# A hybrid SSD and gated-MLP trunk on one core: the first stage by halves of the tokens, in a fixed order

## The chip, the core and the metric

The kernel runs on one NeuronCore of a Trainium2 chip. The metric is the time of one execution on the device in microseconds (us): the median of several runs. One execution was also profiled, and every row shown here is from that execution.

The core's engines each work through their own queue in order: TensorE (PE, matrix products and transposes; its weight loads are PEld), VectorE (DVE), ScalarE (ACT), GpSimd (POOL) and SyncE (SP, which here only issues loads and stores). PE writes its results to PSUM, eight banks of 128 x 512 float32.

## What is computed

Two layers on 512 tokens of width 1024, all in float32. The first layer mixes by a state-space scan (SSD), the second by a gated MLP; each is followed by a SwiGLU and a gated embedding. The change lies in the first projection of the first layer:

```python
def rmsnorm(x, w, eps=RMS_EPS):
    return x * rsqrt(mean(x * x, axis=-1) + eps) * w

def ssd_mixer(u, w_in, ...):                 # u = rmsnorm(h, norm_mix[0])
    zxbcdt = u @ w_in                        # 1024 -> 2048 (z) + 4096 (x, B, C) + 32 (dt)
    xbc = silu(causal_dwconv(xbc, conv_w, conv_b))
    dt = softplus(dt + dt_bias)
    a = -exp(a_log)
    y = ssd_scan(xs, dt, a, bm, cm) + xs * d_skip[:, None]     # chunks of 128 tokens, 8 groups
    return gated_rmsnorm(y, z, norm_w) @ w_out

h = x
for i in range(2):
    h = h + mixer_i(rmsnorm(h, norm_mix[i]))
    h = h + swiglu(rmsnorm(h, norm_ffn[i]), ...)
    h = h + sigmoid(rmsnorm(h, ple_gate_norm[i]) @ ple_w_gate[i]) * rmsnorm(p[i] @ ple_w_proj[i], ple_norm[i])
return rmsnorm(h, final_norm)
```

## The kernel before

**Products in three.** To keep float32 accuracy at the fast rate, each operand is split in a high part, rounded to a short float32 form by a copy on ACT, and a low part, the difference, made by a subtraction. A product is then three on PE (`mm3`): high by high (L265), weights' high by x's low (L266), weights' low by x's high (L267). Weights come in units of 128 columns for all 1024 rows: `wraw` as loaded, `whi` and `wlo` after the split (L68 on ACT, L70 on DVE, for the first two units on POOL), with three buffers each of `whi` and `wlo` and two of `wraw`. The activations are eight blocks of 128 rows by 512 tokens, `xh` and `xl` (tags xh0 to xh7, xl0 to xl7).

**The first stage.** x is loaded as four chunks of 128 tokens in two pieces each (`gh`, L222 and L223), then the first weights, then a row of small loads, all on SP's queue. For each chunk DVE sums the squares of one piece (L381), ACT of the other (L382); a square root and a reciprocal give `rtok`, one over the norm of each token. PE transposes x into seven banks and `on_rows` spreads rtok over the rows (`rs`, copied by DVE at L303). Then for each of the eight blocks: DVE scales the transposed x by the norm's weight and by rs (L395), ACT makes xh (L397) and keeps the unscaled block as the residual H (L400), DVE or POOL makes xl (L398). With these, PE makes the products of units 0 and 1, which are group 0's B and C; then it transposes three sets of small parameters to columns (`to_columns`, L364), makes dt's 32 columns from xh and xl by the unsplit weights `wdt` (the tile u, L627), and goes on with unit 2, group 0's first block of xs.

**After it.** One unit's products (24 of 128x512) follow another: xs, xs, z, z of group 0, then six units for each of the groups 1 to 7. Between them stand the pieces of the scan, started by counts (`tock`, twice in a unit). `decays` makes the cumulative sums from dt; `spread` transposes them, writes them to DRAM and group 0's scan loads them back broadcast to all rows (`csb` and `e`, L502 and L505). POOL multiplies e by C (L578) and makes xdd from xdt (L571), which PE reads for the states (L583).

**Who orders.** The code is traced once and a scheduler then orders each engine's instructions by priority and by estimates of their times; tiles are assigned to buffers and waits follow from the reads and writes. A block under `tc.high_priority` (the weights' splits are) moves ahead.

## Time and profile before

| what | value |
|---|---|
| median of 3 runs | 1576.19 us (1574.93 to 1577.48) |
| the profiled execution's own time | 1578.61 us |
| span of its trace, first to last instruction | 1576.9 us |
| PE busy | 1551.4 us, 98% of the span |
| DVE, ACT, POOL busy | 908.5 (58%), 643.7 (41%), 281.6 us (18%) |

The profiled execution is 2.4 us over the median, and 1.7 us of its time lie outside the span. [...] Of the span's first slice of 39 us PE is busy for seven tenths, of nearly all others for nine or more.

### The profile page before, as it was taken

Reading aid. Unit: us, or ns where it says so; the run is one execution under the profiler, and the core shown is the slowest. Engines: PE = TensorE matmul, PEld = TensorE weight load, DVE = VectorE, ACT = ScalarE, POOL = GpSimd, SP = SyncE. Lnnn points to the kernel's source line nnn. Section 1 sums busy time; section 2 is a strip of 40 time slices with the busy share of each in tenths; the row PEclk is TensorE's granted clock in tenths of the full one; section 3 lists DMA queues with packets and bytes.
Section 4 is the critical chain, followed back from the end, with each engine's and each line's share of the span. In section 5 each row is a group of like instructions: output and inputs, shape, how many; then the busy total and the mean of one; then the engine's idle time right before and its main releaser. Section 6 shows DMA issues by size and latency. Waiting matters only on the chain.

```text
span 1576.9 us, 18208 instructions
## 1 busy us (share of the span) xinstructions
PE 1551.4 (98%) x7348; PEld 1282.0 (81%) x7348; DVE 908.5 (58%) x1226; ACT 643.7 (41%) x843; POOL 281.6 (18%) x219
## 2 busy tenths in 40 slices
PE   7999999999999999999999999999999999999997
PEld 5878788888878788888888888888888888888886
DVE  5679895699886433433456647435554354433445
ACT  5556653466454222222344534323443242212336
POOL 2032220122254101100124200202221001101020
PEclk8999999999999999999999999999999999999999
DMA  6453453434424233233232333332232332333231
GB/s 181 113 139 108 127 127 104 111 121 121 140 81 133 87 102 107 81 107 96 78 120 81 107 92 102 96 111 88 87 107 83 105 101 86 107 92 95 81 107 54
DMA packets 151364, 164.15 MB, mean 104 GB/s; under 512 B 5320, under 2 KB 133872, under 8 KB 151280
## 3 DMA queue, kind: packets, MB, share of 16 engines
q1 hardware_dynamic: 149648, 157.74, 33.2%
q0 software_dynamic: 1600, 5.24, 1.2%
q8 instruction: 57, 0.93, 0.2%
q14 instruction: 27, 0.22, 0.1%
q10 hardware_dynamic: 32, 0.01, 0.0%
HBM read 160.75 MB, written 2.23 MB: 103 GB/s over the span
## 4 chain that ended last, share of the span: by engine, by line
PE 90%; DVE 5%; DMA 2%; ACT 1%; POOL 1%; issue 1%; SPq 0%; ACTq 0%; DVEq 0%; POOLq 0%
PE ps L265 28%; PE ps L266 28%; PE ps L267 28%; PE ps L872 1%; DVE wlo L70 1%; PE ps L527 1%; PE ps L260 1%; DVE acc L451 1%; DVE csb L511 1%; PE ps L583 1%; DMA csb<-cs_dram 1%; PE ps L529 1%; POOL sq L350 0%; DVE rs L283 0%; DVE csb L576 0%
## 5 line engine op out<-in xcount | busy, mean ns | idle before, releaser
L68 ACT ACTIVATE whi<-wraw 128x1024 fp32r<-128x1024 f32 (+1 forms) x270 | 279.0, 1038 | 698.6 <-PE ps L266 616.3
L265 PE MATMUL ps<-xh,whi 128*128 128x512 f32 x1120 | 442.4, 395 | 1.9 <-ACT h L400 1.9
L266 PE MATMUL ps<-xl,whi 128*128 128x512 f32 x1120 | 437.8, 391 | 2.9 <-DVE xl L398 2.0
L267 PE MATMUL ps<-xh,wlo 128*128 128x512 f32 x1120 | 437.8, 391 | 0.0
L70 DVE TENSOR_TENSOR wlo<-wraw,whi 128x1024 fp32r<-128x1024 f32 (+1 forms) x268 | 326.3, 1222 | 98.1 <-ACT whi L68 96.7
L265 PE MATMUL ps<-gh,whi 128*128 128x512 f32 x784 | 306.3, 391 | 0.0
L266 PE MATMUL ps<-gl,whi 128*128 128x512 f32 x784 | 305.0, 389 | 0.0
L267 PE MATMUL ps<-gh,wlo 128*128 128x512 f32 x784 | 304.9, 389 | 0.0
L265 PEld LDWEIGHTS ps<-xh,whi 128*128 128x128 f32 x1120 | 211.4, 189 | 48.9 <-issue 2.8
L266 PEld LDWEIGHTS ps<-xl,whi 128*128 128x128 f32 x1120 | 211.4, 189 | 47.3 <-DVE xl L398 2.5
L267 PEld LDWEIGHTS ps<-xh,wlo 128*128 128x128 f32 x1120 | 211.1, 188 | 44.5
L265 PEld LDWEIGHTS ps<-gh,whi 128*128 128x128 f32 x784 | 147.2, 188 | 30.7 <-issue 0.3
L606 DVE TENSOR_TENSOR h<-h,ps 128x512 f32<-128x512 f32 x88 | 60.0, 685 | 194.5 <-PE ps L267 194.4
L267 PEld LDWEIGHTS ps<-gh,wlo 128*128 128x128 f32 x784 | 147.2, 188 | 30.6
L266 PEld LDWEIGHTS ps<-gl,whi 128*128 128x128 f32 x784 | 147.3, 188 | 30.0
L752 POOL TENSOR_TENSOR zs<-zs,rs 128x512 f32<-128x512 f32 x44 | 74.1, 1687 | 545.9 <-ACT zs L751 545.9
L758 DVE TENSOR_TENSOR xsT<-ps,zs 128x512 f32<-128x512 f32 x44 | 30.4, 691 | 126.6 <-PE ps L267 117.9
L749 DVE TENSOR_TENSOR acc<-ps,rs 128x512 f32<-128x512 f32 x44 | 30.4, 690 | 108.2 <-PE ps L267 108.2
L350 POOL TENSOR_TENSOR sq<-sq,sq 128x512 f32<-128x512 f32 x43 | 65.7, 1528 | 131.3 <-ACT sq L347 129.4
L265 PE MATMUL ps<-whi,gh 128*128 128x512 f32 (+1 forms) x200 | 76.4, 382 | 0.0
L266 PE MATMUL ps<-wlo,gh 128*128 128x512 f32 (+1 forms) x200 | 76.2, 381 | 0.0
L267 PE MATMUL ps<-whi,gl 128*128 128x512 f32 (+1 forms) x200 | 76.1, 381 | 0.0
(293 smaller groups left out, 1419.6 us busy)
## 6 DMA issues: line engine op xcount, KB each, us to landing
wraw<-in_ffn_w_gate_dram SPq DMA_DIRECT2D x22, 1024.0 KB, 5.4
wraw<-in_ffn_w_up_dram SPq DMA_DIRECT2D x22, 1024.0 KB, 5.4
wraw<-in_ssd_w_in_dram SPq DMA_DIRECT2D x16, 1024.0 KB, 5.4
wraw<-in_ffn_w_down_dram SPq DMA_DIRECT2D x16, 1024.0 KB, 5.2
wraw<-in_gmlp_w_in_dram SPq DMA_DIRECT2D x16, 1024.0 KB, 5.5
wraw<-in_ssd_w_in_dram SPq DMA_DIRECT2D x16, 512.0 KB, 4.7
csb<-cs_dram SPq DMA_DIRECT2D x32, 256.0 KB, 4.4
wraw<-in_ple_w_gate_dram SPq DMA_DIRECT2D x8, 1024.0 KB, 5.1
```

The costliest lines, as they stand in the source:

```text
L68: nc.scalar.activation(hi, src, AF.Copy)
L70: (nc.vector if n > 1 else nc.gpsimd).tensor_tensor(lo, src, f32(hi), op=ALU.subtract)
L260: nc.tensor.transpose(ps, src, ident)
L265: mm(ps, wh, xh, start=start, stop=False)
L266: mm(ps, wh, xl, start=False, stop=False)
L267: mm(ps, wl, xh, start=False, stop=stop)
L350: nc.gpsimd.tensor_tensor(sq, sq, accum, op=ALU.add)
L451: stt(a[:, d:], ps[:, : S - d], pcols[:, 0, j * 32 + b : j * 32 + b + 1], a[:, d:], op0=ALU.mult, op1=ALU.add)
L606: tt(H[m], H[m], ps, op=ALU.add)
L749: tt(a, ps, rs, op=ALU.mult)
L752: nc.gpsimd.tensor_tensor(s, s, rs, op=ALU.mult)
L758: tt(t, ps, gate[m], op=ALU.mult)
```

## The change

The first stage is written anew, in an order that holds as written on every engine.

- **Halves of the tokens.** x's first two chunks are loaded, then the first weights, then the other two chunks, and unit 2's and 3's weights at once behind them. Scaling, xh, xl and H are made for tokens 0 to 255 for all eight blocks and then for tokens 256 to 511, in 128x256 pieces; the products of units 0 and 1 likewise, 96 of 128x256 for 48 of 128x512. The weights' low parts of these two units are made in halves, three on DVE and one on POOL.
- **A fixed order.** `in_order` ties each instruction in its block to the one traced before it on the same engine. Instructions from outside the block can still be put between them.
- **Idle transposes.** `warm(n)` has PE transpose the identity into a bank that nobody reads: 8 at the start, 4 and 8 around the row factors.
- **dt from H.** dt's products read H, without the norm, by weights that DVE has scaled by the norm's weights (L749): 8 products for 16. The token factor rtok is multiplied in afterwards, in `softplus`, which runs in the middle of the first xs unit.
- **Moved.** Small loads go to ACT's and POOL's queues; p's load goes from the start to group 2; the copy of d, the third set of columns, and `spread` (to the middle of group 1's first unit) are placed elsewhere; a square-root is done at the start, so that ACT's table for it is there.

```diff
+@contextmanager
+def in_order(tc):
+    traced = tc.nc.cur_bb.bb.instructions
+    last = traced[-1]
+    yield
+    prev = {}
+    for i in traced[next(k for k in reversed(range(len(traced))) if traced[k] is last) + 1 :]:
+        if i.engine in prev:
+            tc.add_manual_dep(i, prev[i.engine].name, mybir.DependencyInfo(
+                mybir.DependencyClass.NoSync, mybir.DependencyReason.DATA), reason="in_order")
+        prev[i.engine] = i
...
-            (nc.vector if n > 1 else nc.gpsimd).tensor_tensor(lo, src, f32(hi), op=ALU.subtract)
+            nc.vector.tensor_tensor(lo, src, f32(hi), op=ALU.subtract)
...
         x_tok.append((a, b))
-    W._load(0)
+        if c == 1:
+            W._load(0)
+    W._load(1)
...
-        q.dma_start(out=rowB[dst[0] : dst[1]], in_=src)
+        nc.gpsimd.dma_start(out=rowB[dst[0] : dst[1]], in_=src)
...
-    for c in range(NCH):
-        one = slice(c, c + 1)
...
-        for k in range(KD - 1):
-            tr_x(xT[k], k, c)
-    rs = on_rows(rtok, nc.vector.tensor_copy)
-    for k in range(KD):
...
+    def x_sums(c):
         stt(slot("e6"), x_tok[c][0], 1.0 / DM, x_tok[c][0], op0=ALU.mult, op1=ALU.mult, accum_out=ss2[:, c, 0:1])
         act(slot("e7"), x_tok[c][1], AF.Square, scale=1.0 / 32, accum_out=ss2[:, c, 1:2])
-        tt(ss[:, one], ss2[:, c, 0:1], ss2[:, c, 1:2], op=ALU.add)
+        tt(ss[:, c : c + 1], ss2[:, c, 0:1], ss2[:, c, 1:2], op=ALU.add)
...
+    def x_scale(hf, k):
+        src, cols = x_part(hf, k)
...
+        stt(tmps[k][:, cols], src, pcolN(k), rs0[:, cols], op0=ALU.mult, op1=ALU.mult)
+        act(Xh[k][:, cols], tmps[k][:, cols], AF.Copy)
+
+    def x_lo(hf, k, engine):
+        cols = slice(hf * HT, (hf + 1) * HT)
+        engine.tensor_tensor(Xl[k][:, cols], tmps[k][:, cols], f32(Xh[k][:, cols]), op=ALU.subtract)
+
+    def x_keep(hf, k):
+        src, cols = x_part(hf, k)
+        act(H[k][:, cols], src, AF.Copy)
...
+    def products(hf, n, k):
+        cols = slice(hf * HT, (hf + 1) * HT)
+        _, wh, wl = units[n]
+        mm3(first[n][:, cols], wh[:, k], wl[:, k], Xh[k][:, cols], Xl[k][:, cols], k == 0, k == KD - 1)
+
+    with in_order(tc):
+        warm(8)
+        to_columns(3, rowN, 16)
+        for c in range(2):
+            x_sums(c)
+            x_transpose(0, c, 0, KD)
+        x_rms(0)
+        x_rms(1)
+        warm(4)
+        x_rows(0)
+        warm(8)
+        unit_hi(0)
+        x_scale(0, 0)
+        x_lo(0, 0, G_)
+        unit_lo(0, V_, 0, 4)
...
+        for c in (2, 3):
+            x_transpose(1, c, 4, KD)
+        W.taken = 2
+        for k in range(KD):
+            x_scale(1, k)
+            x_lo(1, k, V_ if k in (0, 3, 6) else G_)
+            if k == 3:
+                W._split(2)
+            x_keep(1, k)
+            for n in range(2):
+                products(1, n, k)
...
+        to_columns(0, rowA, P)
+        to_columns(1, rowB, P)
+
+        tt(wdt, wdt, pcols[:, 3, :KD].unsqueeze(2).to_broadcast([P, KD, 32]), op=ALU.mult)
+    for m in range(2):
+        bc(m, first[m])
...
-        for n, x_ in enumerate((Xh, Xl)):
-            for j in range(4):
-                mm(ps[j * 32 : (j + 1) * 32], wdt[:, 2 * j + k], f32(x_[2 * j + k]), start=k + n == 0, stop=k + n == 2)
+        for j in range(4):
+            mm(ps[j * 32 : (j + 1) * 32], wdt[:, 2 * j + k], H[2 * j + k], start=k == 0, stop=k == 1)
...
+    gemm(1, KD, Xh, Xl, xs, tick=half)
...
     def tock():
+        if now[0] == 13:
+            spread()
...
-            if g == 1 and b == 0:
-                spread()
+            if g == 2 and b == 0:
+                load_p(0, [slot("e6"), slot("e7")])
```

Three places show how instructions stand now. The first is POOL's queue in the first stage, before: the two loads of p, the low parts of the two weight units, and three low parts of x.

```order
L254 DMA e6_82_470<-in_p_dram 128x2x256
L254 DMA e7_83_471<-in_p_dram 128x2x256
L70 TENSOR_TENSOR wlo0_283<-wraw0_113,whi0_282 128x1024
L70 TENSOR_TENSOR wlo1_287<-wraw0_113,whi1_286 128x1024
L398 TENSOR_TENSOR xl3_46_238<-e3_44_235,xh3_45_237 128x512
L398 TENSOR_TENSOR xl5_54_254<-e5_52_251,xh5_53_253 128x512
L398 TENSOR_TENSOR xl7_63_275<-acc_61_272,xh7_62_274 128x512
```

After, POOL's queue there has seven rows for the first half of the tokens, and the first of the second half behind them (e0 to e5 and acc are the scaled x).

```order
L440 TENSOR_TENSOR xl0_28_209<-e0_26_207,xh0_27_208 128x256
L440 TENSOR_TENSOR xl1_34_225<-e1_32_223,xh1_33_224 128x256
L665 TENSOR_TENSOR wlo0_205<-wraw0_105,whi0_204 128x512
L440 TENSOR_TENSOR xl3_42_246<-e3_40_244,xh3_41_245 128x256
L440 TENSOR_TENSOR xl5_50_279<-e5_48_277,xh5_49_278 128x256
L440 TENSOR_TENSOR xl6_58_311<-acc_56_309,xh6_57_310 128x256
L440 TENSOR_TENSOR xl7_62_318<-acc_60_316,xh7_61_317 128x256
```

The whole units have gone to DVE in three of four halves, and POOL has more and smaller subtractions of x.

The second place is the end of the stage on DVE. Before, the low parts of units 3 and 4 stand between the copies of the transposed parameters (pcols), and dt's result is copied (csb) behind them; nothing that dt's products read is made here.

```order
L398 TENSOR_TENSOR xl6_58_262<-acc_56_259,xh6_57_261 128x512
L365 COPY pcols_134<-ps_67_340 128x128
L70 TENSOR_TENSOR wlo3_391<-wraw1_280,whi3_390 128x1024
L70 TENSOR_TENSOR wlo4_398<-wraw2_384,whi4_397 128x1024
L365 COPY pcols_134<-ps_68_343 128x128
L365 COPY pcols_134<-ps_69_346 128x56
L628 COPY csb_75_365<-ps_76_366 128x512
```

After, the scaling of dt's weights (L749; u is wdt's tile) is the last row of the fixed order, and the same two low parts have been put ahead of it.

```order
L440 TENSOR_TENSOR xl6_58_311<-acc_56_309,xh6_57_310 128x256
L435 SCALAR_TENSOR_TENSOR acc_60_316<-ps_68_359,pcols_135,rs_14_139 128x256
L744 COPY cbm_3_94<-d2_125 16x128
L384 COPY pcols_135<-ps_69_453 128x128
L384 COPY pcols_135<-ps_70_456 128x128
L89 TENSOR_TENSOR wlo3_490<-wraw1_116,whi3_489 128x1024
L89 TENSOR_TENSOR wlo4_497<-wraw2_399,whi4_496 128x1024
L749 TENSOR_TENSOR u_13_127<-u_13_127,pcols_135 128x256
```

What dt's products read is thus made behind the low parts of units 3 and 4.

The third place is the end of the stage on PE, after: the last products of units 0 and 1 (banks ps_30 and ps_31), two transposes of parameters, dt's products by u from H, and the first product of xs.

```order
L284 MATMUL ps_31_216<-xh7_61_317,whi1_220 128x256
L285 MATMUL ps_31_216<-xl7_62_318,whi1_220 128x256
L286 MATMUL ps_31_216<-xh7_61_317,wlo1_221 128x256
L383 MATMUL ps_69_453<-ident_73,Btok_2_93 128x128
L383 MATMUL ps_70_456<-ident_73,cbm_3_94 128x128
L758 MATMUL ps_76_475<-h0_29_210,u_13_127 32x512
L758 MATMUL ps_76_475<-h2_39_236,u_13_127 32x512
...
L758 MATMUL ps_76_475<-h7_63_319,u_13_127 32x512
L284 MATMUL ps_79_500<-xh0_27_208,whi2_401 128x512
```

Between the last product of the stage and dt's there are only the two transposes, and xs stands behind dt, as it did before.

## Rows read from the trace of the kernel before

**Rows 1.** The page's part 1: engine, busy us, share, instructions.

```profile
PE 1551.4 (98%) x7348; PEld 1282.0 (81%) x7348; DVE 908.5 (58%) x1226; ACT 643.7 (41%) x843; POOL 281.6 (18%) x219
```

**Rows 2.** Waits of PE: who waited for whom, us in total, times, longest.

```profile
PE ps L266 <- DVE xl L398: 2.0, 1, 2.0
...
PE ps L583 <- POOL xdd L571: 1.6, 1, 1.6
```

**Rows 3.** Busy us by stretch: PE, PEld, DVE, ACT, POOL; clock, DMA share, GB/s.

```profile
11.00:14.00 3.00, 1.74 (x9) 0.88 (x8) 1.92 (x7) 2.17 (x6) 2.35 (x3) 0.97 1.06 268
14.00:19.00 5.00, 1.11 (x3) 0.51 (x3) 3.91 (x5) 2.93 (x5) 3.92 (x2) 0.50 0.57 130
19.00:24.00 5.00, 5.00 (x12) 3.91 (x13) 5.00 (x9) 4.29 (x9) 1.64 (x2) 0.50 1.08 357
24.00:32.00 8.00, 8.00 (x36) 6.53 (x35) 2.31 (x3) 3.67 (x7) 2.38 (x2) 1.00 0.06 17
```

**Rows 4.** Timeline of the first stage: start, duration, engine, line, operation, [idle before <-releaser].

```profile
7.61 0.63 ACT L382 ACTIVATE e<-gh 128x512 f32<-128x512 f32 x1 [2.13 <-DMA gh<-in_x_dram]
...
11.25 1.60 POOL L254 DMA_DIRECT2D e<-in_p_dram  x2 [9.01 <-DVE ss L383]
11.31 0.19 ACT L382 ACTIVATION_READ_ACCUMULATOR e<-gh 128x1 f32 x1
...
12.63 0.69 DVE L303 COPY rs<-ps 128x512 f32<-128x512 f32 x1 [0.42 <-PE ps L260]
13.26 4.66 POOL L70 TENSOR_TENSOR wlo<-wraw,whi 128x1024 fp32r<-128x1024 f32 x2 [0.41 <-ACT whi L68]
...
13.86 1.06 ACT L68 ACTIVATE whi<-wraw 128x1024 fp32r<-128x1024 f32 x1 [0.69 <-DMA wraw<-in_ssd_w_in_dram]
...
15.82 2.19 DVE L238 COPY cbm<-d 16x128 f32<-16x128 f32 x1 [1.06 <-DMA d<-in_ssd_d_dram]
...
18.78 0.80 PE L266 MATMUL ps<-xl,whi 128*128 128x512 f32 x1 [2.01 <-DVE xl L398]
...
31.84 0.39 PE L267 MATMUL ps<-xh,wlo 128*128 128x512 f32 x1
...
32.57 1.07 PE L627 MATMUL ps<-xh,u 128*32 128x512 f32 x8
...
36.14 0.50 PE L265 MATMUL ps<-xh,whi 128*128 128x512 f32 x1
```

**Rows 5.** PE's timeline near the kernel's end, first and last of 36 products.

```profile
1562.30 0.28 PE L265 MATMUL ps<-whi,gh 128*128 128x256 f32 x1
...
1566.49 0.28 PE L267 MATMUL ps<-whi,gl 128*128 128x256 f32 x1
```

**Rows 6.** Groups by form, whole run: count | busy us, mean ns of one | idle before.

```profile
L540 DVE SCALAR_TENSOR_TENSOR u<-xsT,pcols,ps 128x256 f32<-128x256 f32 x32 | 14.6, 471 | 1.9 <-PE ps L529 1.9
L584 DVE COPY prev<-ps 128x256 f32<-128x256 f32 x8 | 3.3, 416 | 0.0
L271 DVE TENSOR_TENSOR gl<-xsT,gh 128x512 fp32r<-128x512 f32 x22 | 15.0, 680 | 0.7 <-ACT gh L270 0.7
L70 DVE TENSOR_TENSOR wlo<-wraw,whi 128x1024 fp32r<-128x1024 f32 x244 | 302.2, 1242 | 96.9 <-ACT whi L68 96.2
L963 ACT ACTIVATE sq<-xh 128x256 f32<-128x256 f32 x1 | 0.4, 400 | 0.0
L965 POOL TENSOR_TENSOR xh<-xh,csb 128x256 f32<-128x256 f32 x2 | 1.4, 724 | 48.3 <-ACT sq L963 47.9 <-DVE rtf L904 0.4
```

**Rows 7.** Timelines of POOL and DVE, 180 to 184 us.

```profile
180.76 1.29 POOL L578 TENSOR_TENSOR e<-e,CT 128x512 f32<-128x512 f32 x1 [1.79 <-DMA e<-cs_dram]
...
180.88 1.45 DVE L541 TENSOR_TENSOR u<-u,zs 128x256 f32<-128x256 f32 x1
...
183.50 0.41 DVE L541 TENSOR_TENSOR u<-u,zs 128x256 f32<-128x256 f32 x1
```

**Rows 8.** POOL's timeline ahead of the states' products.

```profile
84.06 2.04 POOL L578 TENSOR_TENSOR e<-e,CT 128x512 f32<-128x512 f32 x1 [1.04 <-DMA e<-cs_dram]
```

More of the change, by code (lines that the diff above doesn't have):

```diff
@@ L1 @@
-from contextlib import ExitStack
+from contextlib import ExitStack, contextmanager
 import concourse.bass as bass
@@ L224, in trunk @@
         x_tok.append((a, b))
-    W._load(0)
+        if c == 1:
+            W._load(0)
+    W._load(1)
     q = nc.sync
-    q.dma_start(out=rowA, in_=ssd_conv_w[0].rearrange("j (b q) -> (j b) q", q=P))
+    qa = nc.scalar
+    qa.dma_start(out=rowA, in_=ssd_conv_w[0].rearrange("j (b q) -> (j b) q", q=P))
     nc.vector.memset(rowB[:32], 0.0)
@@ L372, in trunk, with warm @@
     rtok = cp.tile([P, NCH, 1], F32, name="rtok")
-    to_columns(3, rowN, 16)
-    xT = [bank() for _ in range(KD - 1)]
-    def tr_x(ps, k, c):
-        tr(ps[:, c * P : (c + 1) * P], x_tok[c][k // 4][:, (k % 4) * P : (k % 4 + 1) * P])
-    for c in range(NCH):
-        one = slice(c, c + 1)
+    HT = S // 2
+    rs0 = work("rs")
+    xT, tmps = {}, {}
+    def warm(n):
+        for _ in range(n):
+            tr(idle[:, :P], ident)
+    idle = bank()
+    def x_sums(c):
         stt(slot("e6"), x_tok[c][0], 1.0 / DM, x_tok[c][0], op0=ALU.mult, op1=ALU.mult, accum_out=ss2[:, c, 0:1])
@@ L389, in trunk, with x_transpose @@
-    for k in range(KD):
-        if k == KD - 1:
-            xT.append(bank())
-            for c in range(NCH):
-                tr_x(xT[k], k, c)
-        t = slot(f"e{k}") if k < 6 else work("acc")
-        stt(t, xT[k], pcolN(k), rs, op0=ALU.mult, op1=ALU.mult)
-        Xh[k], Xl[k] = xslot(k)
-        act(Xh[k], t, AF.Copy)
-        (nc.gpsimd if k in (3, 5, 7) else nc.vector).tensor_tensor(Xl[k], t, f32(Xh[k]), op=ALU.subtract)
-        H[k] = slot(f"h{k}")
-        act(H[k], xT[k], AF.Copy)
+    def x_transpose(hf, c, k0, k1):
+        for k in range(k0, k1):
+            if c % 2 == 0 and k % 2 == 0:
+                xT[hf, k // 2] = bank()
+            o = (k % 2) * HT + (c % 2) * P
+            tr(xT[hf, k // 2][:, o : o + P], x_tok[c][k // 4][:, (k % 4) * P : (k % 4 + 1) * P])
@@ L609, in trunk, with unit_hi @@
     bc, xs, z = in_proj(0)
-    def first_bc(m, ps):
-        if m == 0:
-            to_columns(0, rowA, P)
-            to_columns(1, rowB, P)
-            to_columns(2, rowC, 56)
-        bc(m, ps)
-    gemm(2, KD, Xh, Xl, first_bc, outer=2, ahead=0)
-    alog = work("Btok")[:, :32]
-    q.dma_start(out=alog, in_=ssd_a_log.partition_broadcast(P).rearrange("q o h -> q (o h)"))
+    V_, G_ = nc.vector, nc.gpsimd
+    first, units = [], []
+    def unit_hi(n):
+        units.append(W.begin(n))
+        act(units[n][1], units[n][0], AF.Copy)
@@ new lines, in unit_lo @@
+    def unit_lo(n, engine, k0, k1):
+        src, hi, lo = (t[:, k0:k1] for t in units[n])
+        engine.tensor_tensor(lo, src, f32(hi), op=ALU.subtract)
+    def products(hf, n, k):
+        cols = slice(hf * HT, (hf + 1) * HT)
+        _, wh, wl = units[n]
+        mm3(first[n][:, cols], wh[:, k], wl[:, k], Xh[k][:, cols], Xl[k][:, cols], k == 0, k == KD - 1)
+    tc.keep_in_program_order(act(cp.tile([P, 1], F32, name="eps_"), eps6, AF.Sqrt))
+    with in_order(tc):
+        warm(8)
+        to_columns(3, rowN, 16)
+        for c in range(2):
+            x_sums(c)
[9 more added lines that the diff above has]
+        unit_lo(0, V_, 0, 4)
+        first.extend((bank(), bank()))
+        products(0, 0, 0)
+        unit_hi(1)
+        x_scale(0, 1)
+        x_lo(0, 1, G_)
+        products(0, 0, 1)
+        x_scale(0, 2)
+        unit_lo(0, G_, 4, 8)
+        x_lo(0, 2, V_)
+        products(0, 0, 2)
+        x_scale(0, 3)
+        x_lo(0, 3, G_)
+        products(0, 0, 3)
+        unit_lo(1, V_, 0, 4)
+        x_scale(0, 4)
+        x_lo(0, 4, V_)
+        products(0, 0, 4)
+        for k in range(4):
+            products(0, 1, k)
+        x_scale(0, 5)
+        x_lo(0, 5, G_)
+        unit_lo(1, V_, 4, 8)
+        products(0, 1, 4)
+        products(0, 0, 5)
+        products(0, 1, 5)
+        x_sums(2)
+        x_transpose(1, 2, 0, 4)
+        for k in range(4):
+            x_keep(0, k)
+        x_scale(0, 6)
+        x_lo(0, 6, G_)
+        x_scale(0, 7)
+        x_lo(0, 7, G_)
+        x_rms(2)
+        products(0, 0, 6)
+        products(0, 1, 6)
+        x_sums(3)
+        x_transpose(1, 3, 0, 4)
+        x_rms(3)
+        products(0, 0, 7)
+        products(0, 1, 7)
+        for k in range(4, KD):
+            x_keep(0, k)
+        x_rows(1)
+        for c in (2, 3):
[9 more added lines that the diff above has]
+                products(1, n, k)
+        nc.vector.tensor_copy(rowB[96:112].rearrange("b (h e) -> b h e", e=64),
+                              d2[96:112].unsqueeze(2).to_broadcast([16, 2, 64]))
+        to_columns(0, rowA, P)
+        to_columns(1, rowB, P)
+        tt(wdt, wdt, pcols[:, 3, :KD].unsqueeze(2).to_broadcast([P, KD, 32]), op=ALU.mult)
@@ L630, in trunk @@
     ps_dt = bank()
-    for c in range(NCH):
-        tr(ps_dt[:, c * P : (c + 1) * P], dtT[:, c * P : (c + 1) * P])
     def ct(name):
```

88 lines of the change are left out of this document (56 added, 32 removed).

## Prediction, made before the changed kernel was run

> **What bounds the kernel now.** The page's first part comes first: TensorE (PE) is busy for 98% of the span [rows 1]. Where is the rest? The waits of PE give the places: 2.0 us at the first low product of x (L266), and one later stall of 1.6 us at L583, where PE waits for GpSimd's xdd [rows 2]. The stretches show the same: PE is busy 1.74 of 3 us from 11 to 14 and 1.11 of 5 from 14 to 19; from 19 on it has no gap, at a granted clock of 0.50 until 24 and of 1.00 after [rows 3]. So the stage ahead of the first xs product is PE's only loose part of any size, and since PE is the bound behind it, the end moves as the start of that product moves. It starts at 36.14 [rows 4]. That is the number to beat, and I build the new one.
>
> The timeline tells how before gets there [rows 4]: VectorE (DVE) copies the row factors at 12.63; at 15.82 its little copy of d takes 2.19 us, because GpSimd (POOL) is at its two subtractions of weight units until 17.92, and the first low part of x comes so late that PE's products run without a gap from 18.78 only. They end behind 31.84, dt's 32 records run from 32.57, and xs starts at 36.14.
>
> **Prices.** A 128x256 product takes 0.12 us (36 of them between 1562.30 and 1566.49) [rows 5]. On DVE a 128x256 scaling out of PSUM takes 0.47 and a copy 0.42; a subtraction of half a weight unit 0.68 (a 128x512 row) and of a whole one 1.24 [rows 6]. ACT's 128x256 pass takes 0.40, which I use for xh and, slightly less, for the H copies; POOL's 128x256 operation 0.72 [rows 6]. A 128x256 DVE subtraction takes 0.41 [rows 7]. An instruction starts when the one ahead of it on its engine and what it reads are done, 0.05 later across engines; back to back, DVE and ACT gain 0.07 to 0.1.
>
> **Start of the stage, at full clock.** The first four pieces of x are issued first as before, so ACT's Square of chunk 1 still starts at 7.61. In before the small steps from the last Square's end (11.50) to DVE's copy of the factors (12.63) take 1.1 [rows 4]; from 8.3 they end at 9.5. Copy 0.42, scaling 0.47, xh 0.40 and hops: first product at 11.0. The weights must be there. In before their second half landed at 13.86, behind eight pieces of x [rows 4]; now it is behind four, and I take 11.0.
>
> **First half.** DVE's queue sets the pace: seven more scalings, three halves of weight units, two subtractions, one sum of chunk 2. With what they wait for on ACT, scaling 7 ends at 18.0. ACT has put four H copies ahead of xh6, so xh7 ends at 18.5; POOL subtracts 6 and 7 until 19.7; products 6, chunk 3's transposes and products 7 end at 21.0.
>
> **Second half.** Row factors, copy, scaling and xh again: first product at 22.9. Subtraction 0 stands ahead of scalings 1 to 3 on DVE, ACT then does xh1 to xh3 with two H copies until 25.4 and splits unit 2 until 26.4. DVE's low part of unit 2 waits for that and stands ahead of scaling 4, so DVE is at 27.7 there, scaling 4 ends at 28.1 and block 4's first product starts at 28.5: PE has waited 1.8. Scaling 7 is behind subtraction 6, which waits for xh6; xh7 ends at 30.9, POOL's subtraction at 31.7, the last product at 32.4. So the early start is eaten: 32.4 against before's 32.1.
>
> **The tail.** dt's products now read wdt scaled by the norm's weights (L749). On DVE that scaling stands behind the low parts of units 3 and 4 (the order's second pair of rows). whi3 may only be written when PE has read whi0 for the last time (32.1), takes 1.06 (33.2), then 1.24 twice (35.5) and 0.4 for wdt: dt starts at 36.0. PE has nothing else in its queue: 3.5 us idle. dt takes half of before's 36.14 - 32.57 = 3.57, thus 1.8: xs starts at 37.8. **Term 1: +1.7 us.** My prices may be off by some 0.04 over the thirty steps of the path: 0.5 to 2.9.
>
> **Term 2, DVE beside POOL.** The rows: a 128x256 DVE operation with both inputs in SBUF takes 0.41 alone and 1.45 when POOL's has begun 0.12 earlier; it ends 0.28 behind POOL's end (180.76 + 1.29 = 182.05) [rows 7]. So it waits the POOL instruction out. POOL shows the reverse: 2.04 where its sisters take 1.29 [rows 7, 8]. Before had three POOL subtractions beside DVE's while PE was at half clock; the new first half has seven on POOL beside nine such DVE ones (three weight halves, two subtractions, two chunk sums with their small adds). Laid into the schedule above: DVE's wlo1 loses 0.9 behind POOL's half of wlo0, POOL's xl3 0.7 behind wlo1, chunk 2's sum 0.8 behind xl5, POOL's xl7 0.7 behind chunk 3's sum, chunk 3's small sum 0.6 behind xl7. What reaches the end of the first half is 2.4, and 0.4 more in the second, where subtractions 3 and 6 wait. **+2.8 us.** Where no two meet it is 0.
>
> [...]
>
> **Term 3, the clock.** Before, the granted clock went to 0.50 behind a stretch with PE busy 1.74 of 3.00, and came back once PE had been busy without a break from 19 to 24 [rows 3]. After has two such stretches: 11 to 15, with about a dozen products of 0.12 in 4 us, and the 3.5 us ahead of dt. A fall in the first half costs little, since PE catches up while it waits for DVE. A fall ahead of dt makes dt's 1.8 into 3.6 and slows the first xs products. I take **+1.8**; bounds 0 and 4.5 (both, with several xs products and some of the first half's thirty queued products at half rate). The inserted transposes fill only PE's time until about 11.
>
> **Term 4, the later stall.** The spread of the decays now stands in the middle of group 1's first unit, 12 products or some 2.7 us (36 in 8 us [rows 3]) earlier against the same L583. There xdd was late by 1.6, because the broadcast rows landed late (POOL's third e product waited for DMA at 84.06 [rows 2, 8]). **-1.6**; bounds -1.6 and 0.
>
> The other edits cost nothing: the small loads moved to ACT's and POOL's queues are issued while these wait for x (POOL's five, at 0.8 each by the two for p at 11.25 [rows 4], are out by 6; were they not, its first subtraction at 11 would be later by the rest); p's loads go to group 2, where POOL has gaps; softplus has one DVE product more, under the xs products, which need nothing of it; its transposes stand behind the 14th xs product, and DVE reaches their copy about 4.7 behind wdt, PE 5.0 (cover gone: a few tenths).
>
> **Sum:** 1.7 + 2.8 + 1.8 - 1.6 = +4.7 us. Against the profiled execution's 1578.61 that is 1583.3. That execution is 2.4 over the median; the median goes from 1576.19 to **1580.9 us**, slower by 0.30%. A measurement of this kernel tells about 0.2%, 3.2 us, from no change.
>
> **Rivals.**
> *No change* (1576.3): DVE's and POOL's subtractions happen not to meet and the clock stays up; terms 1 and 4 are left, +0.1. For it: my schedule has slots of tenths between them. Against it: POOL needs 6 x 0.72 + 1.29 = 5.6 us and DVE's SBUF work 3 x 0.68 + 2 x 0.41 + 2 x 0.69 = 4.2 in the same ten, in a fixed order with the scalings between.
> *Faster* (1571.4): the zigzag between DVE and ACT costs nothing, because each finds its inputs ready. DVE's queue alone then sets the stage: 7.1 us behind 10.0, 1.9 for the row factors, 8 x 0.40 + 3 x 0.35 + 1.24 = 5.5, and 3 for the last block and its wait: products end at 27.5, xs starts at 32.9: -3.2 - 1.6 = -4.8. It decides if xs starts before 34.6. Against it: wlo2 and subtractions 0, 3, 6 each wait for an ACT result of the same block.
> *The load order doesn't do what it says* (1583.4): if the weights' second half still lands near 13.9, xh1, behind whi1 on ACT, is 2.5 late with all behind it: +2.5 on my sum. Against it: a megabyte fewer ahead of it.
>
> **How the numbers follow.** Forecast 0.57, no change 0.20, faster 0.13, late weights 0.10. The forecast's own range is 1577 to 1585: with half of term 2 and no clock it falls under the bound. So of its 0.57, 0.47 is slower and 0.10 same; of no change, 0.17 is same and 0.03 faster. Slower 0.57, same 0.27, faster 0.16. The range 1574.0 to 1585.3 leaves out the faster case, some of the next, and the worst of the clock with late weights: 0.19.
>
> **What would show it.** Right: first product near 11; PE idle about 3 us ahead of dt with DVE at the low parts of units 3 and 4; DVE or POOL subtractions of over 1 us in the first half; clock 0.50 in dt; xs at 42 or so; no wait at the states' products. Wrong: xs before 37, or dt straight behind the last product.

## The result, and the profile after

The changed kernel takes **1585.29 us** (median of 4 runs, 1584.23 to 1585.85) against 1575.83 for the kernel before (median of 4 runs): a ratio of 1.0058, 95% interval 1.0041 to 1.0075, thus 9.5 us slower. Its profiled execution took 1585.28 with a span of 1583.1. TensorE's waits, as in [rows 2]:

```profile
PE ps L758 <- DVE u L749: 3.2, 1, 3.2
PE ps L284 <- ACT xh L436: 3.1, 4, 1.7
PE ps L285 <- POOL xl L440: 2.8, 6, 0.8
PE ps L298 <- DVE rs L290: 1.9, 2, 1.5
...
PE ps L627 <- POOL x L616: 0.8, 1, 0.8
...
PE ps L627 <- POOL xdd L615: 0.6, 1, 0.6
```

The 2.0 us at the first low product are gone; in their place stand 3.2 ahead of dt's products (L758), and shorter waits at xh and xl all through the stage. The same stage by stretches, with the columns of [rows 3]:

```profile
10.00:12.00 2.00, 0.79 (x4) 0.48 (x3) 1.67 (x4) 1.62 (x4) 0.89 (x1) 0.99 1.05 381
12.00:18.80 6.80, 5.56 (x22) 4.70 (x21) 5.49 (x11) 3.44 (x12) 4.54 (x4) 0.50 0.69 199
...
24.50:32.40 7.90, 5.23 (x31) 4.11 (x31) 4.62 (x9) 4.77 (x14) 2.59 (x4) 1.00 0.00 0
32.40:35.90 3.50, 3.22 (x16) 3.15 (x16) 1.11 (x3) 1.02 (x4) 1.03 (x2) 0.51 0.00 0
35.90:39.20 3.30, 0.72 (x6) 0.48 (x5) 2.62 (x4) 3.27 (x4) 0.00 (x0) 1.00 0.02 5
39.20:42.70 3.50, 2.88 (x16) 0.59 (x16) 3.50 (x7) 0.07 (x1) 0.00 (x0) 0.51 0.93 251
```

In this stage TensorE's granted clock, 1.00 when full, is 0.50 or 0.51 three times: in the first half, in the second half's last blocks, and in dt's products. Each time TensorE had waited just before (it was busy for 0.79 of 2.00 us, for 5.23 of 7.90 and for 0.72 of 3.30). The timeline from the wait ahead of block 4 to xs, with [rows 4]'s columns:

```profile
30.70 0.38 PE L284 MATMUL ps<-xh,whi 128*128 128x256 f32 x1 [1.73 <-ACT xh L436]
...
33.41 0.22 DVE L744 COPY cbm<-d 16x128 f32<-16x128 f32 x1
...
35.94 2.00 ACT L88 ACTIVATE whi<-wraw 128x1024 fp32r<-128x1024 f32 x2 [1.84 <-PE ps L285]
36.12 0.28 PE L286 MATMUL ps<-xh,wlo 128*128 128x256 f32 x1
...
37.07 2.36 DVE L89 TENSOR_TENSOR wlo<-wraw,whi 128x1024 fp32r<-128x1024 f32 x2
...
39.34 0.42 DVE L749 TENSOR_TENSOR u<-u,pcols 128x256 f32<-128x256 f32 x1
39.82 3.31 PE L758 MATMUL ps<-h,u 128*32 128x512 f32 x16 [3.20 <-DVE u L749]
43.05 0.50 PE L284 MATMUL ps<-xh,whi 128*128 128x512 f32 x1
```

L758 is dt's products and L284 behind it the first of xs. ACT may write the next weights only when TensorE has read whi0 for the last time (it sits idle for 1.84 us until then); VectorE makes both low parts, and only then the scaled wdt (u). The first xs product starts at 43.05 instead of 36.14 [rows 4]: 6.9 us are lost before it, as against the profiled execution of the kernel before.

### The profile page after: what moved, and what is told of

It reads as the page before. It is cut to its first block, busy times and chain, and to the rows that moved or that the text cites. A ratio compares the mean times of both kernels' runs of the same rounds, so it can differ in the third digit from the quotient of the medians.

```text
span 1583.1 us, 18361 instructions
## 1 busy us (share of the span) xinstructions
PE 1555.3 (98%) x7400; PEld 1286.5 (81%) x7400; DVE 905.2 (57%) x1241; ACT 643.6 (41%) x858; POOL 289.6 (18%) x231
## 4 chain that ended last, share of the span: by engine, by line
PE 89%; DVE 5%; ACT 2%; DMA 2%; POOL 1%; issue 1%; SPq 0%; DVEq 0%; POOLq 0%; ACTq 0%
PE ps L284 28%; PE ps L285 28%; PE ps L286 28%; DVE wlo L89 1%; DMA csb<-cs_dram 1%; PE ps L1019 1%; PE ps L571 1%; DVE csb L555 1%; PE ps L279 1%; DVE csb L620 1%; PE ps L573 1%; DVE acc L495 1%; ACT whi L88 1%; PE ps L627 1%; POOL sq L369 0%
## 5 line engine op out<-in xcount | busy, mean ns | idle before, releaser
L284 PE MATMUL ps<-xh,whi 128*128 128x512 f32 (+1 forms) x1136 | 445.8, 392 | 3.1 <-ACT xh L436 3.1
L285 PE MATMUL ps<-xl,whi 128*128 128x512 f32 (+1 forms) x1136 | 441.5, 389 | 3.8 <-POOL xl L440 2.8
L286 PE MATMUL ps<-xh,wlo 128*128 128x512 f32 (+1 forms) x1136 | 440.7, 388 | 0.0
L284 PE MATMUL ps<-gh,whi 128*128 128x512 f32 x784 | 306.3, 391 | 0.0
L284 PEld LDWEIGHTS ps<-xh,whi 128*128 128x128 f32 x1136 | 214.9, 189 | 50.4 <-ACT xh L436 4.3
L285 PEld LDWEIGHTS ps<-xl,whi 128*128 128x128 f32 x1136 | 214.9, 189 | 48.3 <-POOL xl L440 4.2
L286 PEld LDWEIGHTS ps<-xh,wlo 128*128 128x128 f32 x1136 | 214.9, 189 | 43.7
L284 PEld LDWEIGHTS ps<-gh,whi 128*128 128x128 f32 x784 | 147.2, 188 | 30.7 <-issue 0.3
L284 PE MATMUL ps<-whi,gh 128*128 128x512 f32 (+1 forms) x200 | 76.4, 382 | 0.0
```

The source lines that it names most:

```text
L284: mm(ps, wh, xh, start=start, stop=False)
L285: mm(ps, wh, xl, start=False, stop=False)
L286: mm(ps, wl, xh, start=False, stop=stop)
```

## The experiments

Each time is a median; ratios, with their 95% intervals, are against the kernel before as timed beside each run (its medians there 1575.6 to 1575.9). A timeline is one execution's, and its time can lie one to two us off the median.

**Early scaling (wdt_early).** One line is moved.

```diff
+        tt(wdt, wdt, pcols[:, 3, :KD]..., op=ALU.mult)
         nc.vector.tensor_copy(rowB[96:112]..., d2[96:112]...)
         to_columns(0, rowA, P)
         to_columns(1, rowB, P)
-        tt(wdt, wdt, pcols[:, 3, :KD]..., op=ALU.mult)
```

> The changed kernel with one line moved: the scaling of wdt stands ahead of the copy of d, so ahead of the low parts of units 3 and 4 on VectorE, where that engine is idle from 33.6 to 36.6 us. Theory (dt waits only because its scaled weights stand behind those low parts): dt starts right behind the two to_columns, at 36.5 instead of 39.8, TensorE has no gap there, the granted clock does not fall behind it, dt takes 1.7 instead of 3.2, and the first xs product starts at 38.3 instead of 43.05: the time is 4.7 us below the changed kernel's 1585.3, about 1580.6, some 5 above the kernel before. Rival 1 (the clock falls anyway, because of the thin stretch ahead of the last block): xs at 39.9, time 1582.1. Rival 2 (units 3 and 4 are needed at once, so the wait only moves to the second xs unit): dt at 36.5, but a gap of 3 us ahead of the xs products of the second unit, time as the changed kernel's.

Measured: **1579.55** (ratio 1.0025, 1.0015 to 1.0036), 5.7 under the changed kernel. The timeline:

```profile
33.37 0.41 DVE L744 TENSOR_TENSOR u<-u,pcols 128x256 f32<-128x256 f32 x1
...
36.78 1.92 PE L757 MATMUL ps<-h,u 128*32 128x512 f32 x16
37.30 2.36 DVE L89 TENSOR_TENSOR wlo<-wraw,whi 128x1024 fp32r<-128x1024 f32 x2
...
38.63 0.50 PE L284 MATMUL ps<-xh,whi 128*128 128x512 f32 x1
```

The scaling fills a hole on VectorE, dt stands right behind the last product and takes 1.85 us (36.78 to 38.63) instead of 3.23 (39.82 to 43.05), and the low parts behind it are in time for xs. The theory holds; both rivals fall. The time fell by 1.0 more than forecast: xs comes 4.4 earlier, and the waits of 0.8 and 0.6 us at the states' products (L627) are not in this trace either.

**The gap filled (gap_filled).**

```diff
+        warm(28)
         tt(wdt, wdt, pcols[:, 3, :KD]..., op=ALU.mult)
```

> The changed kernel with 28 more transposes of the identity (about 3.1 us at full clock) in the gap of TensorE ahead of dt's products; nothing else is moved, dt still waits for the scaled wdt until 39.8. Theory (the half clock in dt comes from TensorE's own idling ahead of it): the granted clock stays at 1.00 from 36 on, dt takes 1.7 instead of 3.2, xs starts at 41.5, the time is 1.5 us under the changed kernel's 1585.3. Rival (the fall comes from the thin second half of the stage, before the gap): the clock is 0.50 in dt as before, xs at 43 and the time as the changed kernel's.

Measured: **1582.17** (1.0042, 1.0030 to 1.0055). By stretches, the filled gap and then dt:

```profile
36.00:39.50 3.50, 3.43 (x32) 3.19 (x30) 3.17 (x6) 2.97 (x4) 0.00 (x0) 1.00 0.07 17
39.50:41.40 1.90, 1.83 (x16) 0.42 (x16) 1.90 (x4) 0.00 (x0) 0.00 (x0) 1.00 0.97 277
```

The granted clock stays at 1.00 from 36.0 to 41.4, dt starts at 39.57 and xs at 41.43, 1.86 us for dt instead of 3.23: so it was TensorE's idling ahead of dt that slowed it. The time fell by 3.1 and not 1.5. Of the rest the trace tells only where it may lie: behind xs it has no wait at the states' products and 0.7 instead of 1.9 us at L298. But this execution is 1.7 under its run's median, so that the filling removed those waits is not shown.

**One input out of PSUM (one_sbuf_input).** The low parts and sums named below are made of other values here, so the kernel's result is not the layer's; the operations stay. The inserted transposes write all four quarters of the bank that is read instead.

```diff
+        stt(slot("e6"), x_tok[c][0] if c < 2 else idle, ...)
...
+        tt(ss[:, c : c + 1], ss2[:, c, 0:1] if c < 2 else idle[:, :1], ...)
...
+        src = idle[:, :HT] if engine is nc.vector and hf == 0 else tmps[k][:, cols]
-        engine.tensor_tensor(Xl[k][:, cols], tmps[k][:, cols], ...)
+        engine.tensor_tensor(Xl[k][:, cols], src, ...)
...
+        if engine is V_:
+            src = idle.rearrange("p (a b) -> p a b", b=src.shape[2])
```

> The changed kernel, in whose first half every VectorE operation with two inputs in SBUF (three low parts of weight halves, two low parts of x, the sums of chunks 2 and 3 with their small adds, and the low part of unit 2 is left as it is) reads one of its two inputs from a PSUM bank instead, in the same shape, place and with the same waits: the values of these low parts and sums are not the reference's. GpSimd's work is unchanged. Theory (a VectorE operation with two SBUF inputs and a GpSimd operation exclude each other): VectorE's 128x512 ones are back at 0.68 and the 128x256 ones at 0.42, GpSimd's 128x256 subtractions back at 0.72 and its weight half at 0.7 to 1.3; the products of the first half end 2 us earlier than 22.7, at 20.6 or so, and xs starts about 2 us earlier than 43.05; time about 1583.3. Rival 1 (the first half is slow because TensorE is at half clock from 12 to 19): the durations shrink, but the half ends at 22.2 or later and xs starts at 42.6 or later. Rival 2 (GpSimd is slow for itself): its durations stay over 1 us.

Measured: **1583.22** (1.0049, 1.0037 to 1.0062). VectorE beside GpSimd, first in the changed kernel (a row marked x2 holds two operations; the first row is scaling 0 and the last but one holds scalings 6 and 7):

```profile
9.71 0.48 DVE L435 SCALAR_TENSOR_TENSOR e<-ps,pcols,rs 128x256 f32<-128x256 f32 x1
...
13.15 1.46 POOL L665 TENSOR_TENSOR wlo<-wraw,whi 128x512 fp32r<-128x512 f32 x1
13.79 1.37 DVE L665 TENSOR_TENSOR wlo<-wraw,whi 128x512 fp32r<-128x512 f32 x1
14.57 1.17 POOL L440 TENSOR_TENSOR xl<-e,xh 128x256 fp32r<-128x256 f32 x1
...
18.17 0.49 DVE L406 TENSOR_TENSOR ss<-ss 128x1 f32<-128x1 f32 x1
...
18.59 0.86 DVE L435 SCALAR_TENSOR_TENSOR acc<-ps,pcols,rs 128x256 f32<-128x256 f32 x2
...
19.59 1.88 POOL L440 TENSOR_TENSOR xl<-acc,xh 128x256 fp32r<-128x256 f32 x2 [0.94 <-ACT xh L436]
```

and the same seven in the experiment:

```profile
10.49 0.48 DVE L435 SCALAR_TENSOR_TENSOR e<-ps,pcols,rs 128x256 f32<-128x256 f32 x1
...
13.45 1.28 POOL L668 TENSOR_TENSOR wlo<-wraw,whi 128x512 fp32r<-128x512 f32 x1
13.75 0.68 DVE L668 TENSOR_TENSOR wlo<-ps,whi 128x512 fp32r<-128x512 f32 x1
14.69 0.72 POOL L441 TENSOR_TENSOR xl<-e,xh 128x256 fp32r<-128x256 f32 x1
...
17.24 0.15 DVE L406 TENSOR_TENSOR ss<-ps,ss 128x1 f32<-128x1 f32 x1
...
17.31 0.87 DVE L435 SCALAR_TENSOR_TENSOR acc<-ps,pcols,rs 128x256 f32<-128x256 f32 x2
...
18.65 1.43 POOL L441 TENSOR_TENSOR xl<-acc,xh 128x256 fp32r<-128x256 f32 x2 [1.26 <-ACT xh L436]
```

With one input in PSUM neither engine holds the other up here: VectorE's half unit takes 0.68 instead of 1.37 us, GpSimd's subtraction 0.72 instead of 1.17. What the two engines lose to each other in this way is called the lock from here on; the runs show its price in such durations, and not what makes it. From scaling 0's start to scaling 7's end VectorE takes 7.69 us (10.49 to 18.18) where the changed kernel takes 9.74 (9.71 to 19.45): 2.05 us for the lock in the first half. The products of this half gained as much (first to last product 9.7 instead of 11.8 us), but there TensorE's products, where nothing held them up, also stood 0.12 us apart, in the changed kernel 0.21 until 18.6, so VectorE's queue is the better price of the lock. In this execution the 0.21 came later, from 30.3 to 33.7, dt took 3.57, and xs started at 41.69, 1.4 earlier than in the changed kernel; the median is 2.1 lower.

**dt on H alone (dt_on_h).** In the kernel before:

```diff
+    tt(wdt, wdt, pcols[:, 3, :KD]..., op=ALU.mult)
     gemm(2, KD, Xh, Xl, first_bc, outer=2, ahead=0)
...
-                mm(ps[...], wdt[:, 2 * j + k], f32(x_[2 * j + k]), ...)
+            mm(ps[...], wdt[:, 2 * j + k], H[2 * j + k], ...)
...
+    tt(v, v, rtok.to_broadcast([P, NCH, 32]), op=ALU.mult)
```

> The kernel before with one part of the change alone: dt's products read H and a wdt scaled by the norm's weights (scaled on VectorE where its queue has it, ahead of the first stage's end), the row factors and the bias are applied behind the transposes. Theory (dt's half of the products is a real gain of 1.8 us that the changed kernel loses to the wait for wdt): dt takes 1.8 instead of 3.6 us, xs starts 1.8 us earlier than 36.14, at 34.4, and the time is 1.5 to 2 us under the kernel before, about 1574. Rival 1 (the sooner start of xs meets a later unit of weights, since units 3 and 4 wait for the same last reads): TensorE waits behind dt or behind the first xs unit and the time is that of the kernel before. Rival 2 (the one operation more on VectorE and the moved scaling delay a low part of x): the last product ends later than 32.1 and the time is the same or slower.

Measured: **1574.65** (0.9991, 0.9983 to 1.0000). dt takes 1.85 instead of 3.57, xs starts at 34.22. The median gains 1.1 of the 1.8: the sign is the theory's, at the edge of what the runs tell.

**The spread, forward in the kernel before (spread_early), and back in the changed one (spread_late).**

```diff
     def tock():
+        if now[0] == 13:
+            spread()
...
-            if g == 1 and b == 0:
-                spread()
```

> The kernel before with one part of the change alone: the spread of the decays stands in the middle of group 1's first unit instead of behind it, 2.7 us earlier. Theory (term 4 of the prediction: xdd is late at the states' products because the spread rows land late): the wait of 1.6 us at L583 goes, and nothing else, so the time is up to 1.6 us under the kernel before, about 1574.2. Rival (xdd is late because of what VectorE and GpSimd do between the landing and the products, not because of the landing): the wait stays over 1 us and the time is that of the kernel before.

Measured: **1574.43** (0.9990, 0.9981 to 0.9999), 1.2 less, and the wait at L583 is gone: the theory holds in the kernel before. The same edit undone in the changed kernel:

> The changed kernel with the spread of the decays back behind group 1's first unit, where the kernel before has it. In the kernel before, moving it forward alone took away a wait of 1.6 us at the states' products and 1.2 us of the time; in the changed kernel 0.8 and 0.6 us of wait stand there all the same. Theory (the move is worth as much here, and without it the wait would be 2 to 3 us): the wait at L627 grows to 2 us or more and the time is 1 to 1.6 us over the changed kernel's 1585.3. Rival (in the changed kernel the rows' last loads wait for buffers that VectorE frees, not for the spread, so the move brings nothing): wait and time as the changed kernel's.

Measured: **1584.88** (1.0054, 1.0040 to 1.0068), no difference to the changed kernel that can be told; but both intervals are over 4 us wide, so the times can't tell 1.6 us from nothing either. Its waits of TensorE:

```profile
PE ps L298 <- DVE rs L290: 3.2, 3, 1.5
...
PE ps L627 <- POOL xdd L615: 0.9, 1, 0.9
```

It has 0.9 us at group 0's states' products, where the changed kernel's trace has 0.8, and none of the 0.6 that the changed kernel has at group 1's (127.92). So the wait of 2 us or more that the theory wants is not there, and between these two executions the move brought 0.1. What is late in the changed kernel's own trace, with the move, is VectorE's second xdt, for which GpSimd's x and then TensorE (at 95.13) wait:

```profile
85.87 1.28 POOL L622 TENSOR_TENSOR e<-e,CT 128x512 f32<-128x512 f32 x1 [3.75 <-DMA e<-cs_dram]
85.94 1.30 DVE L555 TENSOR_SCALAR csb<-csb,cs 128x128 f32<-128x128 f32 x1
...
87.82 2.29 DVE L555 TENSOR_SCALAR csb<-csb,cs 128x128 f32<-128x128 f32 x6
88.52 1.32 POOL L622 TENSOR_TENSOR e<-e,CT 128x512 f32<-128x512 f32 x1 [1.36 <-DMA e<-cs_dram]
...
93.75 0.68 DVE L612 TENSOR_TENSOR xdt<-ps,dt 128x512 f32<-128x512 f32 x1
```

From 85.94 on VectorE has no gap until that xdt, and in its queue two small operations on the rows, of 0.28 us alone, take 1.3 each beside GpSimd's e products. The ten traces with the move agree: the four with two such operations (the changed kernel, one_sbuf_input, unit2_late, unit2_behind_d) have a wait of 0.1 to 0.8 at group 0's states' products, the six with one (of 0.8 to 1.3; wdt_early, gap_filled, vector_alone, vector_ordered, and spread_early and before_best from the kernel before) have none. The rival's result holds for the changed kernel, then, but the cause that the traces point to is the lock and not buffers; no run takes the lock away there.

**Unit 2 late (unit2_late), and behind the copy of d (unit2_behind_d).** Both are built on the early scaling.

```diff
             x_lo(1, k, V_ if k in (0, 3, 6) else G_)
-            if k == 3:
-                W._split(2)
...
         tt(wdt, wdt, pcols[:, 3, :KD]..., op=ALU.mult)
+        W._split(2)                                # unit2_late
         nc.vector.tensor_copy(rowB[96:112]..., d2[96:112]...)
+        W._split(2)                                # unit2_behind_d, instead
         to_columns(0, rowA, P)
```

> The run with the early scaling of wdt, with one thing more moved: unit 2 of the weights is split behind the last block of the second half instead of ahead of its block 4. Theory (term 1's gap of 1.73 us ahead of block 4 is the price of that split, which the early start of the stage paid for): the gap goes, the last product ends 2 us earlier than 36.2, dt starts at 34.6, xs at 36.5 instead of 38.6, and the time is 2.1 us under that run's 1579.6, about 1577.5. Rival (three units in a row then stand ahead of the sums of B and C on VectorE, and a later unit comes late): the gap goes but TensorE waits in the xs products, time as with the early scaling alone.

Measured: **1582.98** (1.0048, 1.0036 to 1.0061), 3.4 worse than the early scaling, and not for the rival's reason:

```profile
33.90 3.50 DVE L89 TENSOR_TENSOR wlo<-wraw,whi 128x1024 fp32r<-128x1024 f32 x3 [1.37 <-ACT whi L88]
37.41 0.22 DVE L744 COPY cbm<-d 16x128 f32<-16x128 f32 x1
...
37.73 0.45 PE L383 MATMUL ps<-ident,cbm 128*128 128x128 f32 x1 [3.25 <-issue]
38.11 3.23 PE L756 MATMUL ps<-h,u 128*32 128x512 f32 x16
```

The last product came 2.0 earlier (34.10), but the small copy of d now stood behind three low parts, TensorE's transpose of its rows waited 3.25 us for it, and dt, queued behind, took 3.16 (38.11 to 41.27), at a granted clock of 0.55 from 37.4 to 41.2. (The wait is listed as issue: the releaser is not recorded, but the copy ends 0.1 us ahead.) So the copy was moved:

> The run with unit 2 late once more, with the copy of d ahead of that split on VectorE instead of behind it. There the last product was at 34.1 us instead of 36.1, as expected, but the second to_columns waited for the copy of d, which stood behind the low parts of units 2 to 4, until 37.7, and dt with it. Theory (the gap ahead of dt is made by whatever small operation that TensorE waits for stands behind those low parts, be it wdt or d): no gap ahead of dt, dt at 34.6 at full clock, xs at 36.5, and 2.1 us under the early scaling's 1579.6, about 1577.5. Rival (xs itself now waits for unit 2): dt at 34.6 but xs at 38 or later, time 1579 or more.

Measured: **1577.27** (1.0009, 1.0001 to 1.0018). No gap, dt at 35.10, xs at 36.96, in an execution whose first product came 0.8 later than the early scaling's (11.53). The two medians differ by 2.3, so the split of unit 2 ahead of block 4 was worth about the 1.8 us that term 1 gave it. Dt and xs came 0.5 later than forecast, less than the late start.

**VectorE alone (vector_alone), and in a better order (vector_ordered).** From unit2_late, all low parts of the first stage on VectorE:

```diff
-        x_lo(0, 0, G_)
         unit_lo(0, V_, 0, 4)
+        x_scale(0, 1)
+        x_lo(0, 0, V_)
...
+        x_scale(1, 0)
         for k in range(KD):
-            x_scale(1, k)
-            x_lo(1, k, V_ if k in (0, 3, 6) else G_)
+            if k + 1 < KD:
+                x_scale(1, k + 1)
+            x_lo(1, k, V_)
```

This moves twelve operations to VectorE, seven in the first half and five in the second (the expectations say ten). It changes the order too: each block's scaling now stands ahead of the low part of the block before it.

> The run with unit 2 late, and in it all subtractions of the first stage on VectorE: GpSimd does none of them. Each low part stands one or two scalings behind its own block's scaling, so that it doesn't wait for ScalarE. The lock's price is then gone, and VectorE has ten operations more. By the prediction's prices VectorE's first half is 8 scalings at 0.40, 8 low parts at 0.35, 4 weight halves at 0.6 and 1.7 of sums, 10.1 us from 9.7 on, so its products end near 20.2 instead of 22.7; the second half is 6.5 behind 2.0 for the row factors, ends near 29; dt 1.9; xs near 31 at full clock, 33 at half, against 36.5 with unit 2 late. Theory (GpSimd's help costs more in the lock than it saves): xs between 31 and 33.5, time 1572 to 1575, under the kernel before. Rival (VectorE becomes the bound and the help was worth its price): the first half ends at 22.5 or later, xs at 36 or later, time 1577 or more.

Measured: **1580.41** (1.0031, 1.0020 to 1.0043). Inconclusive on the lock, since two orders of mine spoilt it: the copy of d as above (3.7 us ahead of dt), and a sum of chunk 2 that waited for a Square behind four copies on ACT, with the low part of block 6 behind it (VectorE at 17.93, that low part at 20.20). Both mended:

> The run with VectorE alone, with two orders mended: the copy of d ahead of the split of unit 2 as in the run beside it, and in the first half the sums of chunk 2 ahead of scaling 6 and the copies of H behind both Squares on ScalarE, so that the low parts of blocks 6 and 7 don't wait on VectorE for a Square behind four copies (they stood idle 17.9 to 19.6 and 20.2 for that). Theory (GpSimd's help costs more in the lock than it saves; only the order spoilt the run before): the first half's products end at 20.5, the second half starts at 22.5 and ends at 28.7, dt at 29, xs at 31, or 32.5 where the clock falls; time 1572 to 1574, under the kernel before. Rival (VectorE's ten operations more cost as much as the lock): the second half starts at 24 or later, xs at 33.5 or later, and the time is 1575 or more.

Measured: **1571.44** (0.9971, 0.9961 to 0.9982). TensorE's timeline, first products of both halves, last product, dt, xs:

```profile
10.57 0.39 PE L284 MATMUL ps<-xh,whi 128*128 128x256 f32 x1 [0.62 <-ACT xh L436]
...
23.16 0.39 PE L284 MATMUL ps<-xh,whi 128*128 128x256 f32 x1
...
29.28 0.28 PE L286 MATMUL ps<-xh,wlo 128*128 128x256 f32 x1
...
29.71 1.92 PE L757 MATMUL ps<-h,u 128*32 128x512 f32 x16
31.56 0.50 PE L284 MATMUL ps<-xh,whi 128*128 128x512 f32 x1
```

The second half takes 6.1 us where the changed kernel took 11.6 (24.53 to 36.12), without one wait of TensorE from 23.2 on, and xs starts 11.5 earlier. With twelve operations more VectorE is fast enough by itself: GpSimd's help was not needed, and the rival falls. How much of the gain comes from taking GpSimd out is not shown, since the early wdt, the late unit 2 and the new order of scalings, sums and copies are in it too. Against unit2_behind_d, which has the first two, xs comes 5.4 earlier and the time is 5.8 lower. No run keeps GpSimd's part in the new order. And 2.9 of the 5.4 lie in the second half (9.0 us there, 6.1 here), where the changed kernel shows no price of the lock.

**GpSimd out of the way in the kernel before (before_units_on_vector).** The first two units' low parts go to VectorE, behind its second scaling; the copy of d goes behind the last.

```diff
-            (nc.vector if n > 1 else nc.gpsimd).tensor_tensor(lo, src, f32(hi), op=ALU.subtract)
+            with self.tc.high_priority(offset=60 if n < 2 else 0):
+                nc.vector.tensor_tensor(lo, src, f32(hi), op=ALU.subtract)
...
+    nc.vector.tensor_copy(rowB[96:112]..., d2[96:112]...)
     gemm(2, KD, Xh, Xl, first_bc, outer=2, ahead=0)
```

> The kernel before with two edits alone: the low parts of the first two units on VectorE behind its second scaling instead of on GpSimd, and the copy of d behind the last scaling. Theory (GpSimd's 4.7 us hold VectorE's first low part back): the first low product at 17.8 to 18.2 instead of 18.8, xs at 35 instead of 36.14, time 1 to 2 us under the kernel before. Rival (VectorE's own 2.3 us more cost as much): xs at 36 or later and the time is that of the kernel before, so that the gain of the run with four edits over its parts came from elsewhere.

Measured: **1573.81** (0.9988, 0.9980 to 0.9997). VectorE's rows and the first low product:

```profile
14.94 2.35 DVE L70 TENSOR_TENSOR wlo<-wraw,whi 128x1024 fp32r<-128x1024 f32 x2
17.20 1.29 DVE L401 TENSOR_TENSOR xl<-e,xh 128x512 fp32r<-128x512 f32 x2
...
17.94 0.80 PE L267 MATMUL ps<-xl,whi 128*128 128x512 f32 x1
```

The first low product stands at 17.94 instead of 18.78, xs at 34.69 instead of 36.14, as expected, and the time is 2.0 lower. Part of the 1.45 at xs is one execution's: spread_early, whose first stage is the kernel before's, has its first low product at 18.91 and xs at 35.15. And two edits stand in this run, so it doesn't part the low parts' move from that of the copy of d, which took 2.19 us beside GpSimd [rows 4].

**Four edits to the kernel before (before_best)**: dt on H, the spread forward, and the two edits of the run above.

> The kernel before, with four edits together: dt's products on H (the run above gave 1.1 us under before), the spread in the middle of group 1's first unit, the first two units' low parts on VectorE behind the second scaling instead of on GpSimd, and the copy of d moved behind the last scaling. Theory (GpSimd's 4.7 us at the two units held VectorE's copy of d and first low part until 18.0): the first low part of x is made at 17.1 instead of 18.0, the gap ahead of the first low product shrinks by 0.9, xs starts at 33.4 instead of 36.14, the wait at the states' products goes, and the time is 1575.7 - 1.1 - 0.9 - 1.5 = 1572.2. Rival (VectorE's two more operations delay the later low parts): TensorE waits at the later blocks, xs at 34.5 or later, time 1574 or more.

Measured: **1571.26** (0.9970, 0.9961 to 0.9979), xs at 32.93. The single edits gave 1.1, 1.2 and 2.0; together 4.4. This and vector_ordered beat both kernels, and their medians are equal, though xs starts 1.4 earlier in vector_ordered's trace. So no gain of halves over whole tokens is shown here, but neither kernel is without waits (before_best's TensorE still waits 2.3 us for ACT ahead of its first product).

## Why the prediction was right, step by step

The sign and the mechanism ahead of xs stood; the forecast of +4.7 us was half of what came, 9.5. That 1585.29 still lies within the range, which ends at 1585.3, is luck: most of the missing half lies behind xs, where the prediction counted on a gain.

- **First product**: 11.0 forecast, 10.70 measured. ACT's second unit started at 11.03, so the weights' second half came when I said, and the rival of late weights falls.
- **Term 1.** The wait ahead of block 4 was put at 1.8 and is 1.73; dt's wait behind the low parts of units 3 and 4 at 3.5 and is 3.2. Shown by unit2_behind_d and wdt_early: taking them away gave 2.3 and 5.7 us (the 5.7 with the clock in dt, and with 1.3 that is not ahead of xs).
- **Term 2**, the lock: +2.4 in the first half forecast, 2.05 measured on VectorE's queue. The 0.4 of the second half is not in the trace: there VectorE's low parts of x take 0.42 to 0.49, about the 0.41 of one alone [rows 7]. That half the term might come, as the forecast's range has it, was only my estimate.
- **Term 3**, the clock, was too small: +1.8. dt at half pace cost 1.4 (3.23 against 1.85 in wdt_early, and 1.86 at a granted clock of 1.00 in gap_filled). The fall that I allowed for in the first half and called cheap came there (0.50 from 12.0 to 18.8), but another in the second half's last blocks: 13 products from 33.14 to 35.70 at about 0.21 instead of 0.12, 1.2 in all. Not all of it counts: the last product starts 1.5 behind the end of GpSimd's last low part (34.63), and 0.6 behind it in unit2_late, where the last products stand 0.12 apart; thus 0.9. Together 2.3.
- Terms 1 to 3 had put xs at 42.4; it is 43.05. That this is so near is luck in part: with the lock the schedule had 25.3 for the second half's first product, which came at 24.53, and 9.9 us from there to the last product, which took 11.6 (0.9 of the difference is the clock).
- **Term 4 is the step that failed: -1.6 and no wait at the states' products forecast, waits of 0.8 and 0.6 there measured.** I took the worth of the move from the kernel before, where spread_early shows that it is real (1.2). In the changed kernel spread_late shows 0.4 the other way, inside the noise. The traces with the move that have the wait are those in which two of VectorE's operations on the rows meet GpSimd's, 1.0 us each: term 2's lock, at a place where I hadn't reckoned with it.
- **Behind xs the prediction has no term but that one, and more is lost there.** TensorE's last product starts 1529.4 us behind xs in the changed kernel, 1527.7 in dt_on_h, which has the later stages of the kernel before: 1.7 more, of which 1.3 is the wait at L298 (1.5 against 0.2 at the same place). A wait of 1.2 us or more there is in seven of the nine traces of kernels made from the changed one, and in one of five from the kernel before: its profiled execution, which has 2.1 us at 193.83 and behind it a granted clock of 0.59 from 194 to 198, and whose time lies 2.9 over the median of the later runs. The wait comes and goes from one execution to the next: the two traces without it, gap_filled's and vector_ordered's, are each the fastest execution of their run, 1.7 and 1.6 under its median, and those of one_sbuf_input and spread_late, which have it twice, are 1.8 over. By carrying the 2.4 of before's execution over to the median unchanged, the prediction took the stretch behind xs to be alike in both kernels. What makes the wait more frequent in those made from the changed one stays open; no run was made for it.
- **The sum.** 6.9 ahead of xs and 1.7 behind it are 8.6 of the 9.5, whose interval goes from 6.5 to 11.8. Some 0.4 more lie outside the span (1585.28 less 1583.1, as against 1.7 before). The 6.9 rests on one execution of the kernel before, whose half clock lasted until 24 us [rows 3]; against spread_early, where xs is at 35.15, it is 7.9.
